# Last norm of a hybrid encoder block: the correction diagonal in one operation, gamma read from PSUM

## The chip, the cores and the metric

The kernel runs on one core of a Trainium2 chip. The time is that of the whole program on the device, in microseconds (us), as the median of three runs. Before the change the three runs took 742.75, 742.79 and 743.09 us; the median is 742.79 us.

Five engines run their own instruction streams: PE (TensorE, the matrix multiplier), DVE (VectorE), ACT (ScalarE), POOL (GpSimd) and SP (SyncE, which here only issues transfers). They wait for one another through semaphores. Matrix products land in PSUM, everything else lives in SBUF.

## The reference

One layer of a streaming encoder: two attention branches with gates, an output projection, a norm, a gated MLP with a causal convolution, and a second norm. All is float32, with 512 rows of 1024 values. What matters here is the last line:

```
def layer_norm(x, g, b):
    mu = jnp.mean(xf, axis=-1, keepdims=True)
    var = jnp.mean(jnp.square(xf - mu), axis=-1, keepdims=True)
    return ((xf - mu) * lax.rsqrt(var + LN_EPS)) * g + b
...
        x = layer_norm(DEEPNORM_ALPHA * x + h @ w_ffn_out[layer], ln2_g[layer], ln2_b[layer])
```

## The kernel before

The 512 rows are four blocks of 128 rows, x1[0] to x1[3]; a row lies on a partition, and its 1024 values are the free dimension, split in a left half (0 to 511) and a right half (512 to 1023). The FFN's second product is a scheme of seven half-size products whose partial sums are added to x1 block by block. Each product is made in float32r, as three matmuls of a high and a low part (lines 1060 to 1062). The weight of the last group is called b22_5; ACT makes its high part, whi, at L104, and DVE its low part, wlo, at L113.

Blocks 2 and 3 finish early, block 0 next, and block 1 last, with nothing left to run beside it. So block 1 has its own ending, `finish(1)`. Its left half is final at about 725 us, before its right half. At that moment DVE takes the mean of the left half alone (`near`, L1271) and computes `ahead` = (left half − near) · gamma (L1274). When the right half is there too, the true mean is known (`mv`, L1170), and the left half only needs a correction: (left − mean) · gamma = ahead + (near − mean) · gamma. PE does that sum: an identity matmul puts `ahead` in PSUM (`share_ps`, L1184), and a matmul of gamma with a diagonal matrix, whose diagonal is near − mean (`diag`, L1176), adds the correction (L1186). The two banks of `share_ps` hold quarters 0 and 1 of the row (256 values each).

The order in `finish(1)` is this. DVE makes `mv`, then `off` = −(mean − near), a 128x1 operation, then `diag` = identity · off, then `less` = (right − mean) · gamma into PSUM. POOL computes `rstd` from the variance by a power (L1172). Then come the second passes, value · rstd + beta: quarters 2, 3 and 1 on DVE (L1192, in that order), quarter 0 on ACT (`scaled`, L1188) and POOL (`r`, L1189). Each quarter goes out by its own transfer: quarters 2 and 1 from SP's queue, quarters 3 and 0 from ACT's queue (L1193, L1194). The norms of the other blocks use the same power on POOL in `norm_stats` (L835) and two passes of `scalar_tensor_tensor` on DVE with all tensors in SBUF (L839, L841).

The order of instructions on each engine is set by a scheduler that simulates the program, except where `issue_after` in the code ties one instruction behind another. Buffers rotate in pools with a fixed number of buffers: psB has four PSUM banks, psD (`bank_p`) two, psC (`bank_c`) two.

Of the kernel before, what the change touches and what calls it, by code (L numbers as in the profile page):

```python
# [11 lines left out]
F32 = mybir.dt.float32  # L12
F32R = mybir.dt.float32r
U16 = mybir.dt.uint16
AF = mybir.ActivationFunctionType
ALU = mybir.AluOpType
# [111 lines left out]
def tile_block(ctx: ExitStack, tc: tile.TileContext, xT, xN, w_qi, w_ki, w_t, w_v, w_br, w_o, w_fi, w_fo,  # L128
               bg, cw, rel, onehot, lnp, out):
    nc = tc.nc  # L130
# [4 lines left out]
    def open_pool(name, side=None, **kw):  # L135
        c = tc.tile_pool(name=name, bufs=1, side=side, **kw)
        return c, c.__enter__()

    def padded(pool, shape, dt=F32, **kw):

        n = int(np.prod(shape[1:]))
        t = pool.tile([shape[0], -(-n // 32) * 32], dt, **kw)[:, :n]
        return t if len(shape) == 2 else t.rearrange("p (a b) -> p a b", a=shape[1])
# [15 lines left out]
    def pb(name):  # L159
        return psB.tile([128, 512], F32, tag="B", name=name)  # L160
# [47 lines left out]
    for _ in range(WARM):  # L208
# [3 lines left out]
    ident = cst.tile([128, 128], F32, name="ident")  # L212
# [4 lines left out]
                            base=-383, channel_multiplier=-1)  # L217
# [604 lines left out]
    dc, dp = open_pool("dp", side="right", reuse_waits="tile")  # L822
# [6 lines left out]
    def norm_stats(r, parts):  # L829

        mv = padded(dp, [128, 2], tag="mv", bufs=2, name="mv")
        nc.vector.bn_aggr(mv, parts)
        rstd = padded(dp, [128, 1], tag="rstd", bufs=2, name="rstd")
        nc.vector.tensor_scalar(rstd, mv[:, 1:2], EPS, None, op0=ALU.add)  # L834
        nc.gpsimd.tensor_tensor(rstd, rstd, mhalf, op=ALU.pow)  # L835
        return mv, rstd

    def norm_apply(dst, r, mv, rstd, g, b, c, behind=None):
        nc.vector.scalar_tensor_tensor(dst[:, c], r[:, c], mv[:, 0:1], g[:, c], op0=ALU.subtract, op1=ALU.mult)  # L839
        with tc.issue_after(behind) if behind is not None else nullcontext():  # L840
            return nc.vector.scalar_tensor_tensor(dst[:, c], dst[:, c], rstd, b[:, c], op0=ALU.mult, op1=ALU.add).ins  # L841
# [214 lines left out]
    def product(ps, ops, part, w, c, start, stop):  # L1056

        (h, l), (wh, wl), (slot, a) = ops, w, part
        r = slice(a * 128, a * 128 + 128)
        nc.tensor.matmul(ps, h[:, slot, r], wh[:, c], start=start, stop=False)  # L1060
        nc.tensor.matmul(ps, h[:, slot, r], wl[:, c], start=False, stop=False)  # L1061
        ups["m"] = nc.tensor.matmul(ps, l[:, slot, r], wh[:, c], start=False, stop=stop).ins  # L1062
# [21 lines left out]
    def bank_c(name):  # L1084
        return psC.tile([128, 512], F32, tag="C", bufs=2, name=name)

    def bank_p(name):
        return psD.tile([128, 512], F32, tag="P", bufs=2, name=name)

    P += [bank_p(f"P{a}") for a in range(2)]  # L1090
    for f in range(2, FC):
# [12 lines left out]
        if f == 4:  # L1104
            later = [(dp.tile([128, D], F32, tag=tag, name=f"ln{row}"), row) for row, tag in ((2, "lg"), (3, "lb"))]
            g2, b2 = later[0][0], later[1][0]
# [15 lines left out]
    wc, wp = open_pool("wp", side="right", reuse_waits="tile")  # L1122
# [27 lines left out]
    left, right = slice(0, 512), slice(512, 1024)  # L1150

    def add(j, c, what, stats=None, eng=nc.vector):

        eng.tensor_add(x1[j][:, c], x1[j][:, c], what)
        if stats is not None:
            nc.vector.bn_stats(parts2[j][:, stats], x1[j][:, c])

    def finish(j, behind=None):
        r = x1[j]
        if j != 1:  # L1160
            mv, rstd = norm_stats(r, parts2[j])
            for c in (left, right):
                norm_apply(r, r, mv, rstd, g2, b2, c, behind)
                sent = (nc.scalar if j == 0 else nc.gpsimd).dma_start(out[j * 128:(j + 1) * 128, c], r[:, c])
            if j != 0:
                with tc.issue_after(sent.ins):
                    nc.gpsimd.drain()
            return
        mv = padded(dp, [128, 2], tag="mv", bufs=2, name="mv")
        nc.vector.bn_aggr(mv, parts2[j])  # L1170
        rstd = padded(dp, [128, 1], tag="rstd", bufs=2, name="rstd")
        nc.gpsimd.tensor_tensor(rstd, mv[:, 1:2], mhalf, op=ALU.pow)  # L1172
        off = padded(dp, [128, 1], name="off")
        nc.vector.tensor_scalar(off, mv[:, 0:1], near[:, 0:1], -1.0, op0=ALU.subtract, op1=ALU.mult)
        diag = wp.tile([128, 512], F32, tag="m1", bufs=2, name="diag")[:, :128]
        turned = nc.vector.tensor_scalar(diag, ident, off, None, op0=ALU.mult).ins  # L1176
        less = bank_p("less_ps")
        with tc.issue_after(turned):
            nc.vector.scalar_tensor_tensor(less, r[:, right], mv[:, 0:1], g2[:, right], op0=ALU.subtract, op1=ALU.mult)
        quarters = [slice(256 * n, 256 * n + 256) for n in range(4)]  # L1180
        shares = [bank_c(f"share_ps{n}")[:, :256] for n in range(2)]
        with tc.issue_after(behind):
            for ps, c in zip(shares, quarters):
                nc.tensor.matmul(ps, ident, ahead[:, c], start=True, stop=False)  # L1184
        for ps, c in zip(shares, quarters):
            nc.tensor.matmul(ps, diag, g2[:, c], start=False, stop=True)  # L1186
        scaled = wp.tile([128, 512], F32, tag="m1", bufs=2, name="scaled")[:, :256]
        nc.scalar.activation(scaled, shares[0], AF.Copy, scale=rstd)  # L1188
        nc.gpsimd.tensor_add(r[:, quarters[0]], scaled, b2[:, quarters[0]])  # L1189
        for n, src, eng in ((2, less[:, 0:256], nc.sync), (3, less[:, 256:512], nc.scalar), (1, shares[1], nc.sync)):  # L1190
            c = quarters[n]
            nc.vector.scalar_tensor_tensor(r[:, c], src, rstd, b2[:, c], op0=ALU.mult, op1=ALU.add)  # L1192
            eng.dma_start(out[j * 128:(j + 1) * 128, c], r[:, c])  # L1193
        nc.scalar.dma_start(out[j * 128:(j + 1) * 128, quarters[0]], r[:, quarters[0]])  # L1194
# [3 lines left out]
    def get(key):  # L1198

        w = st.get(key)  # L1200
        while st.used < len(order) and order[st.used][0] in HOLD:
            t = order[st.used][0]
            held[t] = st.get(t)
        return w
# [12 lines left out]
    m1, u2, u3 = [], [], []  # L1217
# [42 lines left out]
    for n in range(2, 6):  # L1260
        group(f"b21_{n}", A12, M2)
        if n == 3:
            for a in range(2):
                finish(2 + a, st.done["b22_0"])
# [5 lines left out]
    near = padded(dp, [128, 2], name="near")  # L1270
# [15 lines left out]
    for n in range(2):  # L1286
# [3 lines left out]
        for i in range(2 * n, 2 * n + 2):  # L1290
            c = slice(i % 2 * 512, i % 2 * 512 + 512)
            product(whole_half, rest_ops[i], (S4, 1), w, c, i == 0, i == parted - 1)
    add(1, right, whole_half)
    held["b22_5"] = get("b22_5")
    for key, w in held.items():
        group(key, S4, M3, (0,), w)
    whole = ups["m"]
    add(0, right, M3[0], 1)
    finish(0)
    for n in range(2):  # L1300
        for key, w in held.items():
            with tc.issue_after(whole):
                last_block(key, w, n)
        add(1, slice(512 + 256 * n, 768 + 256 * n), halves[n], 1 + n)
    finish(1, ups["m"])
    close(wc)
    close(fc)
# [71 lines left out]
```

## Time and profile before

| | before |
|---|---|
| median of three runs | 742.79 us |
| profiled execution | 742.96 us |
| its span, first to last instruction | 741.1 us |
| PE busy | 734.5 us, 99% |
| DVE busy | 569.7 us, 77% |
| ACT busy | 409.0 us, 55% |
| POOL busy | 153.4 us, 21% |
| granted PE clock | 1.0 |

A row of a timeline gives the start in us, the duration in us (for merged rows from the first start to the last end), the engine, the line, the operation, output<-inputs and a count. A q behind an engine's name is its sequencer, which issues transfers. A row of the groups gives busy time in us and the mean of one instruction in ns, and the idle time ahead of it.

### The profile page before, as it was taken

To read this page: it belongs to the slowest core of one execution; us is meant where nothing else is said; L and a number is where in the kernel's file an instruction comes from. 1 tells how busy PE (TensorE), PEld (TensorE's weight loads), DVE (VectorE), ACT (ScalarE), POOL (GpSimd) and SP (SyncE) were. 2 spreads that over 40 slices of the span, in tenths; PEclk is the share of its full clock that TensorE was granted. 3 is DMA by queue.
4 is the path that set the end of the run, shared out by engine and by line. 5 is a ranking of instruction groups with operands and counts; after the bars stand their busy time and mean duration, and the time that the engine had idled before them with its cause. 6 is when DMAs were issued, how large, how long until landed. Compare 5 with 4: busy or idle time off the path is not lost.

```text
span 741.1 us, 9715 instructions
## 1 busy us (share of the span) xinstructions
PE 734.5 (99%) x3445; PEld 615.1 (83%) x3445; DVE 569.7 (77%) x912; ACT 409.0 (55%) x575; POOL 153.4 (21%) x168
## 2 busy tenths in 40 slices
PE   9999999999999999999999999999999999999997
PEld 7888888888888888888889888888888888888886
DVE  5569888999679898568856876686667677668986
ACT  6466867797786688755384443443444344336430
POOL 1002224365753341000100222012101100110011
PEclk9999999999999999999999999999999999999999
DMA  8335977797566464438631554444443444447532
GB/s 281 144 127 202 204 165 173 156 211 174 126 172 164 135 142 122 124 112 263 241 64 50 174 153 150 157 160 145 149 155 115 154 146 149 137 151 279 183 136 86
DMA packets 74959, 117.29 MB, mean 158 GB/s; under 512 B 43736, under 2 KB 44248, under 8 KB 74912
## 3 DMA queue, kind: packets, MB, share of 16 engines
q1 hardware_dynamic: 67536, 94.38, 41.1%
q0 software_dynamic: 5840, 18.38, 10.3%
q10 hardware_dynamic: 1536, 3.93, 2.1%
q8 instruction: 27, 0.44, 0.2%
q14 instruction: 20, 0.16, 0.1%
HBM read 95.93 MB, written 9.98 MB: 143 GB/s over the span
## 4 chain that ended last, share of the span: by engine, by line
PE 98%; DVE 1%; DMA 0%; issue 0%; ACT 0%; POOLq 0%; POOL 0%
PE g_ps L966 16%; PE u_ps L966 16%; PE av_ps L512 3%; PE m L1062 2%; PE m L1061 2%; PE m L1060 2%; PE ga_ps L233 2%; PE ga_ps L234 2%; PE ga_ps L232 2%; PE gb_ps L234 2%; PE gb_ps L232 2%; PE gb_ps L233 2%; PE o_ps L867 2%; PE o_ps L869 2%; PE o_ps L868 2%; PE z_ps L539 1%
## 5 line engine op out<-in xcount | busy, mean ns | idle before, releaser
L104 ACT ACTIVATE whi<-raw 128x1024 fp32r<-128x1024 f32 (+1 forms) x124 | 123.5, 999 | 130.5 <-PE g_ps L966 40.0
L113 DVE TENSOR_TENSOR wlo<-raw,whi 128x1024 fp32r<-128x1024 f32 (+1 forms) x105 | 122.7, 1171 | 36.3 <-ACT whi L104 35.8
L966 PE MATMUL g_ps<-x1h,whi 128*128 128x512 f32 (+1 forms) x184 | 70.1, 381 | 0.0
L966 PE MATMUL g_ps<-x1h,wlo 128*128 128x512 f32 (+1 forms) x184 | 69.9, 380 | 0.0
L966 PE MATMUL g_ps<-x1l,whi 128*128 128x512 f32 (+1 forms) x184 | 69.9, 380 | 0.0
L966 PE MATMUL u_ps<-x1h,whi 128*128 128x512 f32 (+1 forms) x184 | 69.6, 380 | 0.0
L966 PE MATMUL u_ps<-x1h,wlo 128*128 128x512 f32 (+1 forms) x184 | 69.6, 380 | 0.0
L966 PE MATMUL u_ps<-x1l,whi 128*128 128x512 f32 (+1 forms) x184 | 68.9, 380 | 0.0
L981 DVE TENSOR_TENSOR t<-raw 128x512 f32<-128x512 f32 x11 | 7.6, 691 | 42.4 <-DMA raw<-in_w_fo_dram 42.4
L966 PEld LDWEIGHTS g_ps<-x1h,whi 128*128 128x128 f32 x184 | 34.6, 188 | 6.7 <-DVE hF L1036 0.3
L966 PEld LDWEIGHTS g_ps<-x1h,wlo 128*128 128x128 f32 x184 | 34.6, 188 | 6.6
L966 PEld LDWEIGHTS g_ps<-x1l,whi 128*128 128x128 f32 x184 | 34.6, 188 | 6.6
L966 PEld LDWEIGHTS u_ps<-x1h,wlo 128*128 128x128 f32 x184 | 34.6, 188 | 6.5
L966 PEld LDWEIGHTS u_ps<-x1h,whi 128*128 128x128 f32 x184 | 34.6, 188 | 6.5
L966 PEld LDWEIGHTS u_ps<-x1l,whi 128*128 128x128 f32 x184 | 34.3, 188 | 6.6
L567 POOL TENSOR_TENSOR bm<-win,score 128x256 f32<-128x256 f32 (+2 forms) x24 | 28.8, 1229 | 32.6 <-DMA pl<-bm 22.2
L1028 ACT ACTIVATE c<-c,cwt 128x512 f32<-128x512 f32 x22 | 15.9, 724 | 31.0 <-DVE c L1027 30.9
L1022 POOL MEMSET u<- 128x2 f32 x22 | 2.1, 98 | 139.6 <-ACT whi L104 83.0
L1036 DVE TENSOR_TENSOR hF<-g_ps,c 128x512 f32<-128x512 f32 x22 | 15.1, 686 | 16.5 <-PE g_ps L966 15.7
L835 POOL TENSOR_TENSOR rstd<-rstd,mhalf 128x1 f32<-128x1 f32 x7 | 6.8, 965 | 100.0 <-DVE rstd L834 100.0
L424 DVE MAX8 m<-score 128x8 f32<-128x256 f32 (+2 forms) x48 | 26.5, 554 | 0.9
L556 POOL TENSOR_TENSOR beta<-beta,keep 128x1280 f32<-128x1280 f32 x8 | 21.0, 2626 | 25.9 <-DVE keep L553 25.9
(598 smaller groups left out, 2089.8 us busy)
## 6 DMA issues: line engine op xcount, KB each, us to landing
raw<-in_w_fi_dram SPq DMA_DIRECT2D x44, 512.0 KB, 3.3
raw<-in_w_t_dram SPq DMA_DIRECT2D x32, 512.0 KB, 3.6
raw<-in_w_fo_dram SPq DMA_DIRECT2D x26, 512.0 KB, 4.3
wlo<-in_w_t_dram POOLq DMA_DIRECT2D x14, 512.0 KB, 6.0
raw<-in_w_br_dram SPq DMA_DIRECT2D x8, 512.0 KB, 3.8
raw<-in_w_o_dram SPq DMA_DIRECT2D x8, 512.0 KB, 3.8
raw<-in_w_v_dram SPq DMA_DIRECT2D x7, 512.0 KB, 4.4
raw_b<-in_w_fo_dram SPq DMA_DIRECT2D x6, 512.0 KB, 5.1
```

The lines of the kernel that those rows point to most:

```text
L104: self.high = nc.scalar.activation(hi[:, :w], t[:, :w], AF.Copy).ins
L113: self.done[key] = eng.tensor_sub(lo[:, :w], t[:, :w], r32(hi[:, :w])).ins
L232: nc.tensor.matmul(ps[:M], wh[:, c], xh[k], start=(k == 0), stop=False)
L233: nc.tensor.matmul(ps[:M], wh[:, c], xl[k], start=False, stop=False)
L234: ups["proj"] = nc.tensor.matmul(ps[:M], wl[:, c], xh[k], start=False, stop=(k == KC - 1)).ins
L424: nc.vector.max(m8, sc)
L512: nc.tensor.matmul(dst, vt[i][:, h].rearrange("p a d -> p (a d)"), t, start=(n == 0), stop=(n == len(seq) - 1))
L556: nc.gpsimd.tensor_mul(beta, beta, keep[:, 1:ATT + 1])
L567: nc.gpsimd.tensor_add(bm[:, OFF[j]:OFF[j] + N], win[:, 512 - N:512], score[j])
L966: nc.tensor.matmul(ps[:, c], a[:, k * 128:k * 128 + 128], b[:, k, c], start=(k == 0 and a is wh and b is x1h), stop=(n == len(terms) - 1 a ...
L1028: nc.scalar.activation(c, c, AF.Gelu_apprx_tanh, bias=cwt[:, f, 3:4])
L1036: nc.vector.tensor_mul(F[:, o:o + 2].rearrange("p a b -> p (a b)"), gps_, c)
```

## The change

`off` goes, and `diag` becomes one operation: diag = (−identity) · mean + identity · near. Its two tensors are made earlier by ACT: `minus`, the negative identity, in an SBUF buffer of the pool that `ahead` uses, and `base`, the identity times `near`, in a PSUM bank of psD. ACT also copies the right half of gamma into a PSUM bank of psB (`gamma`), and `less` reads it there in place of g2 in SBUF. `base` has the bank that `less` had, and `less` the one of the partial sum `m3_1` that was added to x1 before.

```
-        off = padded(dp, [128, 1], name="off")
-        nc.vector.tensor_scalar(off, mv[:, 0:1], near[:, 0:1], -1.0, op0=ALU.subtract, op1=ALU.mult)
         diag = wp.tile([128, 512], F32, tag="m1", bufs=2, name="diag")[:, :128]
-        turned = nc.vector.tensor_scalar(diag, ident, off, None, op0=ALU.mult).ins
+        turned = nc.vector.scalar_tensor_tensor(diag, minus, mv[:, 0:1], base, op0=ALU.mult, op1=ALU.add).ins
         less = bank_p("less_ps")
         with tc.issue_after(turned):
-            nc.vector.scalar_tensor_tensor(less, r[:, right], mv[:, 0:1], g2[:, right], op0=ALU.subtract, op1=ALU.mult)
+            nc.vector.scalar_tensor_tensor(less, r[:, right], mv[:, 0:1], gamma, op0=ALU.subtract, op1=ALU.mult)
...
     add(1, right, whole_half)
+    minus = wp.tile([128, 512], F32, tag="u2", bufs=2, name="minus")[:, :128]
+    nc.scalar.activation(minus, ident, AF.Copy, scale=-1.0)
+    base, gamma = bank_p("base_ps")[:, :128], pb("gamma_ps")
+    nc.scalar.activation(base, ident, AF.Copy, scale=near[:, 0:1])
+    nc.scalar.activation(gamma, g2[:, right], AF.Copy)
     held["b22_5"] = get("b22_5")
```

DVE's stream in `finish(1)`, before (ln_4290 is gamma, ln_4291 beta, r_3475 block 1; what a row waits for stands in brackets):

```order
L1170 BN_AGGR mv<-parts_1_6009 128x2 [waits DVE_49]
L1174 TENSOR_SCALAR off<-mv,near 128x1 [waits DVE_49]
L1176 TENSOR_SCALAR diag<-ident,off 128x128 [waits DVE_49]
L1179 SCALAR_TENSOR_TENSOR less_ps<-r_3475,mv,ln_4290 128x512
L1192 SCALAR_TENSOR_TENSOR r_3475<-less_ps,rstd,ln_4291 128x256 [waits DVE_49,Pool_49]
L1192 SCALAR_TENSOR_TENSOR r_3475<-less_ps,rstd,ln_4291 128x256
L1192 SCALAR_TENSOR_TENSOR r_3475<-share_ps_6543,rstd,ln_4291 128x256 [waits PE_49]
```

and now:

```order
L1170 BN_AGGR mv<-parts_1_6009 128x2 [waits DVE_49]
L1174 SCALAR_TENSOR_TENSOR diag<-minus,mv,base_ps 128x128 [waits DVE_49,Activation_49]
L1177 SCALAR_TENSOR_TENSOR less_ps<-r_3475,mv,gamma_ps 128x512
L1190 SCALAR_TENSOR_TENSOR r_3475<-less_ps,rstd,ln_4291 128x256 [waits DVE_49,Pool_49]
L1190 SCALAR_TENSOR_TENSOR r_3475<-less_ps,rstd,ln_4291 128x256
L1190 SCALAR_TENSOR_TENSOR r_3475<-share_ps_6547,rstd,ln_4291 128x256 [waits PE_49]
```

The row of `off` is gone, `diag` has a second semaphore to wait for, that of ACT, and the rows behind it keep their order and their waits.

ACT's stream from the high part of the weights b22_0 (`b_0h`) to the end, as a difference (whi_6392 is the high part of b22_5):

```order
 L104 ACTIVATE b_0h<-raw_b_0_6315 128x1024 [waits DMAHW6_49,DVE_49,PE_49]
+L1296 ACTIVATE gamma_ps<-ln_4290 128x512
 L104 ACTIVATE whi_6392<-raw_b_5_6350 128x512 [waits DMAHW0_49,PE_49]
+L1295 ACTIVATE base_ps<-ident,near 128x128 [waits DVE_49]
+L1293 ACTIVATE minus<-ident 128x128
 L1164 DMA out_dram<-r_3474 128x512 [waits DVE_49] x2
```

The copy of gamma has moved ahead of whi, though it stands behind `near` in the code; `base` and `minus` stand between whi and the output transfers of block 0. Of the three only `base` waits, for DVE. On PE, POOL and SP the rows and their order are as before.

## The prediction

> **What bounds the kernel now.** I read the page first, for the engine that sets the pace, then the stages of the end, then the timeline of the last eight microseconds.
>
> ```profile
> PE 734.5 (99%) x3445; PEld 615.1 (83%) x3445; DVE 569.7 (77%) x912; ACT 409.0 (55%) x575; POOL 153.4 (21%) x168
> ```
>
> PE is busy for 99% of the span, so only PE's work, or the stretch at the end where PE has none, can change the time. The change leaves PE's stream alone. The stretches (start:end, length, then busy time of PE, PEld, DVE, ACT, POOL with counts, PE clock, DMA share, GB/s) show where that end is:
>
> ```profile
> 725.00:734.00 9.00, 9.00 (x61) 8.34 (x60) 5.73 (x13) 0.00 (x0) 2.00 (x3) 1.00 0.16 60
> 734.00:738.00 4.00, 2.03 (x9) 1.12 (x7) 3.63 (x10) 0.47 (x1) 1.28 (x2) 1.00 0.36 133
> 738.00:741.00 3.00, 0.00 (x0) 0.00 (x0) 0.00 (x0) 0.00 (x0) 0.00 (x0) 0.95 0.52 172
> ```
>
> Until 734 PE has no gap; from 734 to 738 DVE is busy for 3.63 of 4.00 us and sets the pace; from 738 on only transfers and the closing run. In the middle stretch the DVE rows are:
>
> ```profile
> 734.12 0.41 DVE L1154 TENSOR_TENSOR r<-r,m 128x256 f32<-128x256 f32 x1
> 734.56 0.43 DVE L1156 BATCH_NORM_STATS2 parts<-r 128x6 f32<-128x256 f32 x1
> 735.02 0.24 DVE L1170 BATCH_NORM_AGGREGATE mv<-parts 128x2 f32<-128x18 f32 x1
> 735.30 0.21 DVE L1174 TENSOR_SCALAR off<-mv,near 128x1 f32<-128x1 f32 x1
> 735.54 0.29 DVE L1176 TENSOR_SCALAR diag<-ident,off 128x128 f32<-128x128 f32 x1
> 735.75 0.75 DVE L1179 SCALAR_TENSOR_TENSOR less_ps<-r,mv,ln 128x512 f32<-128x512 f32 x1
> 736.60 0.88 DVE L1192 SCALAR_TENSOR_TENSOR r<-less_ps,rstd,ln 128x256 f32<-128x256 f32 x2
> 737.40 0.47 DVE L1192 SCALAR_TENSOR_TENSOR r<-share_ps,rstd,ln 128x256 f32<-128x256 f32 x1
> ```
>
> and those of the other engines:
>
> ```profile
> 735.88 1.13 PE L1186 MATMUL share_ps<-ln,diag 128*128 128x256 f32 x4 [0.98 <-DVE diag L1176]
> 736.68 0.47 ACT L1188 ACTIVATE scaled<-share_ps,rstd 128x256 f32<-128x256 f32 x1 [18.57 <-PE share_ps L1186]
> 735.41 0.55 POOL L1172 TENSOR_TENSOR rstd<-mv,mhalf 128x1 f32<-128x1 f32 x1 [3.43 <-DVE mv L1170]
> 737.23 0.73 POOL L1189 TENSOR_TENSOR r<-scaled,ln 128x256 f32<-128x256 f32 x1 [1.28 <-ACT scaled L1188]
> 737.12 0.36 SPq L1193 DMA_DIRECT2D out_dram<-r  x1
> 737.90 0.34 SPq L1193 DMA_DIRECT2D out_dram<-r  x1
> 737.99 0.36 ACTq L1194 DMA_DIRECT2D out_dram<-r  x1
> ```
>
> The reader should see two branches behind `mv`. The **DVE branch** is off, diag, less, three second passes, and SP's last transfer at 737.90. The **PE branch** leaves it at diag: PE at 735.88, ACT at 736.68, POOL at 737.23, and ACT's transfer at 737.99, which is the last of the program. The DVE branch has 0.09 us of slack against it. `rstd` is there at 735.41 + 0.55 = 735.96 and isn't last for anyone: DVE's second pass begins at 736.60, 0.10 after less ended, and ACT waits for PE.
>
> **The change part by part.** *off goes.* From off's start to diag's is 735.54 − 735.30 = 0.24 us. The new diag needs `mv` as off did, so I start it at 735.30. Its other wait, ACT's `minus`, is long over (below).
>
> *diag gets dearer.* No such operation of 128x128 is in the trace; larger ones and two others of 128x128 are (group rows: busy, mean ns):
>
> ```profile
> L839 DVE SCALAR_TENSOR_TENSOR r<-r,mv,ln 128x512 f32<-128x512 f32 x12 | 8.4, 742 | 0.0
> L1192 DVE SCALAR_TENSOR_TENSOR r<-less_ps,rstd,ln 128x256 f32<-128x256 f32 x2 | 0.9, 478 | 0.1
> L584 DVE CUSTOM_DVE_ANT_0 lg<-l_ps,win 128x128 f32<-128x128 f32 x8 | 2.3, 283 | 0.0
> L594 DVE TENSOR_SCALAR lg<-lg,rs 128x128 f32<-128x128 f32 x8 | 4.9, 608 | 0.2
> ```
>
> From 512 to 256 elements the cost falls by 264 ns, so from 256 to 128 by 132: 346 ns, and L1192 reads one of its tensors from PSUM, as diag now will. The bounds are 283 ns (L584, one PSUM and one SBUF tensor of this very size) and 608 ns (L594). I take 346, from the same operation. Then diag ends at 735.30 + 0.346 = 735.65, where it ended at 735.54 + 0.286 = 735.83: **−0.18 us** (by the bounds −0.24 to +0.08). PE's first row, 0.05 behind diag, goes from 735.88 to 735.70, and with it ACT, POOL and the last transfer: 737.99 becomes 737.81.
>
> *less on DVE.* It began 0.21 after diag's start, 0.076 before diag's recorded end; the same overlap gives 735.30 + 0.346 − 0.076 = 735.57, also −0.18. It reads gamma from PSUM now. Rows with a PSUM tensor at 512, and the slowest of this operation at that size:
>
> ```profile
> L878 DVE SCALAR_TENSOR_TENSOR r<-r,o_ps 128x512 f32<-128x512 f32 x8 | 5.4, 683 | 6.8 <-PE o_ps L869 6.8
> L415 DVE SCALAR_TENSOR_TENSOR score<-relu,wi,score 128x512 f32<-128x512 f32 x7 | 6.0, 864 | 0.0
> ```
>
> L878 has no pointer scalar, which less has; so I keep less's own 754 ns, with 683 and 864 as bounds. It then ends at 736.32, the second passes start at 736.42, and SP's last transfer is at 737.72. At 864 ns it would be 737.83, 0.02 behind ACT's 737.81: the slack nearly hides it, and the sum would be −0.16. At 683 nothing more is won, since ACT's transfer is last.
>
> *rstd on POOL* starts at 735.41 as before and must now be there by 736.42 (0.18 sooner). The same power elsewhere is dearer:
>
> ```profile
> L835 POOL TENSOR_TENSOR rstd<-rstd,mhalf x7: 923/983/1008, 363.6 to 731.0; 128x1 f32<-128x1 f32 x7
> 730.81 1.40 DVE L839 SCALAR_TENSOR_TENSOR r<-r,mv,ln 128x512 f32<-128x512 f32 x2
> 731.04 0.93 POOL L835 TENSOR_TENSOR rstd<-rstd,mhalf 128x1 f32<-128x1 f32 x1 [4.35 <-DVE rstd L834]
> ```
>
> Seven times it took 0.92 to 1.01 us while DVE ran L839, whose tensors all lie in SBUF; at L1172, beside off and diag, 0.55. The first pass of L839 ends at 730.81 + 0.74 = 731.55 and the power at 731.97, 0.42 later. So the power looks held until a pass over two SBUF tensors is over. In the new order less starts 0.18 nearer to the power, which is where gamma's place counts: with a PSUM tensor less has one SBUF tensor, and so has diag. I take 0.55; even 1.01 would end at 736.42, just in time, so this term is nothing either way.
>
> The Trainium skill has a rule for this, in SBUF — State Buffer, Who interferes with whom: a DVE instruction with two SBUF inputs contends with a GpSimd instruction that reads SBUF, whichever comes first blocks the other to its end, and one with at most one SBUF input doesn't contend. The seven rows of L835 agree with it; by it the new diag and less leave the power alone, and the sum stays. But by it the power at 735.41 should also have held up the old diag, a SBUF to SBUF scaling, until 735.96; diag's row shows 0.29 us. So the rule isn't carried by every row here.
>
> *ACT's three copies.* The timeline rows around them, and last a group row for the size:
>
> ```profile
> 714.76 1.06 ACT L104 ACTIVATE b_0h<-raw_b 128x1024 fp32r<-128x1024 f32 x1 [1.66 <-DVE wlo L113]
> 717.48 0.63 ACT L104 ACTIVATE whi<-raw_b 128x512 fp32r<-128x512 f32 x1 [1.66 <-PE m L1062]
> 724.89 0.17 DVE L1271 BATCH_NORM_AGGREGATE near<-parts 128x2 f32<-128x6 f32 x1
> 728.16 0.39 PE L1060 MATMUL m<-whi,bh 128*128 128x512 f32 x1
> 733.24 1.00 ACTq L1164 DMA_DIRECT2D out_dram<-r  x2
> L587 ACT ACTIVATE lg<-lg,mn 128x128 f32<-128x128 f32 x8 | 3.1, 394 | 0.3 <-DVE mn L584 0.3
> ```
>
> gamma costs what whi of the same shape does, 0.63 us, and falls in the 1.66 us in which ACT sat idle ahead of whi: nothing. Were that cover gone, whi would come 0.63 later, and PE needs it only at 728.16. base waits for near (725.06), and takes with minus about 2 · 0.39 us (estimate from L587's row): both are done by 726.0. Behind them on ACT stand only block 0's transfers at 733.24, 7 us later, and diag needs them at 735.30. Nothing.
>
> **Sum:** −0.18 us. The profiled execution took 742.96 (span 741.1 and 1.86 around it), which becomes 742.78; that execution lies 0.17 above the median, so the median goes from 742.79 to **742.6 us**, −0.02%.
>
> **The rivals.** *A: rstd becomes late* (slower). If DVE's less holds POOL up although gamma is in PSUM, or if the power slips behind it, rstd ends 0.42 after less: 736.32 + 0.42 = 736.74. With the 0.10 gap the second passes start at 736.84, 0.24 later than before, and SP's last transfer moves from 737.90 to 738.14, 0.15 behind the old last one: 742.94. It decides once rstd comes after 736.42, and costs more than the change brings once it comes after about 736.6. For it: the seven long powers. Against it: less has one SBUF tensor, and the power starts 0.16 before it. *B: the end does not move.* The four transfers of 128 KB are what the span ends with, and DMA moves 172 GB/s in the last stretch; if their landing rather than their issue set the end, the time stays 742.8. Against it: the first of them is issued at 737.12, and from 734 to 738 the DMA share is 0.36, so nothing of an earlier stage fills the engines, and all four are issued 0.18 sooner. *C: diag is as slow as L594's row,* 608 ns: +0.08 us, 742.9, and less is late by as much. Against it: L1192 and L839 both put it near 346. *D: the edit does more than I see,* because the old diag or less paid for the power beside them: less's 754 against L839's 742 leaves 0.01 us, so 742.6 at best.
>
> **How the numbers follow.** Forecast (with D, the same time) 0.68; A 0.12; B 0.13; C 0.07. The cases lie within 742.6 to 742.94. The three runs of before spread from −0.04 to +0.30 around their median, and another set of runs need not have the same median. So the range is 742.2 (0.4 under the forecast, for bounds of −0.24 and the spread) to 743.2 (A plus the spread). A measurement of this kernel can tell about 0.2%, 1.5 us, from no change; no case comes near that in either direction, since the whole stretch behind `mv` to the last transfer is only 2.7 us long. Hence: faster by more than 0.2% 0.03, within it 0.95, slower 0.02, where what is left stands for things that the trace doesn't hold.
>
> **What would show it.** In the new profile, counted from `mv`'s start: diag 0.28 later and some 0.35 long; PE's gamma·diag matmul 0.68 later (0.86 before); the first second pass 1.40 later (1.58); ACT's last transfer 2.79 later (2.97). rstd of 0.55 us shows the power free; one near 1.0, ending 0.42 behind less, shows A, and then the idle time ahead of the second pass names POOL. A transfer issued sooner with the same end shows B. A diag above 0.53 us shows C. A gap on PE at 728.16, or whi well after 717.48, would show that ACT's copies aren't hidden, and would make the prediction wrong.

## The result, and the profile after

The changed kernel takes **750.57 us** (median of four, 750.1 to 751.21) against 742.86 for the kernel before (four runs, 742.75 to 743.09): a ratio of 1.010, with a 95% interval of 1.0088 to 1.0113. It is 7.7 us slower. The forecast was 742.6 us and no measurable change.

The profiled execution took 751.21 us, with a span of 749.4. The page's row of busy times:

```profile
PE 742.7 (99%) x3445; PEld 615.5 (82%) x3445; DVE 570.4 (76%) x911; ACT 410.6 (55%) x578; POOL 152.1 (20%) x168
```

PE runs as many instructions as before and is busy for 8.2 us longer, at the same share of 99%; in sum it waited no more, its work took longer. The stretches, cut at the first matmul of the FFN's first product (L966), at the end of its part with matmuls of 256 columns, at its last matmul, and at mv (start:end, length, then busy time of PE, PEld, DVE, ACT, POOL, PE clock, DMA share, GB/s; PEld is PE's loading of weights), before:

```profile
0.00:388.25 388.25, 386.74 (x1846) 325.03 (x1847) 310.02 (x553) 266.90 (x401) 105.57 (x95) 1.00 0.62 167
388.25:402.70 14.45, 14.45 (x111) 13.91 (x110) 7.71 (x13) 5.97 (x8) 1.01 (x3) 1.00 0.09 18
402.70:671.00 268.30, 268.30 (x1187) 222.05 (x1186) 192.54 (x255) 111.17 (x140) 40.48 (x61) 1.00 0.45 149
671.00:735.00 64.00, 63.90 (x302) 53.47 (x301) 56.73 (x84) 24.51 (x27) 5.11 (x7) 1.00 0.51 177
735.00:741.10 6.10, 1.13 (x4) 0.68 (x4) 2.67 (x7) 0.47 (x1) 1.28 (x2) 0.97 0.34 117
```

and after:

```profile
0.00:389.60 389.60, 387.98 (x1847) 325.42 (x1848) 310.49 (x553) 266.89 (x401) 104.17 (x95) 1.00 0.63 166
389.60:404.00 14.40, 14.40 (x110) 13.80 (x109) 7.71 (x13) 6.03 (x8) 1.01 (x3) 1.00 0.09 18
404.00:679.00 275.00, 275.00 (x1188) 222.25 (x1187) 192.92 (x255) 111.70 (x141) 40.51 (x61) 1.00 0.45 146
679.00:743.30 64.30, 64.15 (x302) 53.34 (x300) 56.73 (x84) 25.52 (x30) 5.11 (x7) 1.00 0.52 175
743.30:749.40 6.10, 1.13 (x4) 0.68 (x4) 2.51 (x6) 0.47 (x1) 1.27 (x2) 0.76 0.33 116
```

The last stretch, where every instruction of the change but ACT's copies lies, is 6.10 us long in both; PE's granted clock is lower in it now, but its four matmuls take 1.13 us in both. The loss sits far ahead of it: 6.7 us between about 403 and 679 us, where the same 1187 or 1188 matmuls need 275.0 us in place of 268.3, with PE busy throughout and the granted clock at 1.00; and 0.3 us in the stretch behind. The second stretch, in the main L966's matmuls of 256 columns, hasn't grown. The first stretch is 1.35 us longer in this execution; 0.8 of it is one wait of PE for a late transfer (L234 below). The other two stretches hold 7.0 of the 7.7 us between the medians; what holds the rest this one profile doesn't show. The chain of waits shows one group of 24 matmuls of 512 columns (start, length, line, count), first of before, then of after:

```profile
503.93 5.44 PE u_ps L966 x24
```

```profile
507.56 5.60 PE u_ps L966 x24
```

One of them takes 5.44 / 24 = 227 ns from start to start before, and 5.60 / 24 = 233 ns now. In the groups by line and shape, L966 has six rows of 168 with 512 columns, 1008 matmuls; one row of before and one of after, and the row of the late transfer:

```profile
L966 PE MATMUL u_ps<-x1h,whi 128*128 128x512 f32 x168 | 65.4, 389 | 0.0
```

```profile
L966 PE MATMUL u_ps<-x1h,whi 128*128 128x512 f32 x168 | 66.4, 395 | 0.0
...
L234 PE MATMUL gb_ps<-xh,wlo 128*128 128x512 f32 x64 | 24.9, 392 | 0.8 <-DMA wlo<-in_w_t_dram 0.8
```

All six rows of L966 went from 389 or 390 to 395 ns, and 1008 · 6.6 ns = 6.7 us. The same shape in the projections ahead of it (L234) is still at 392. So something about the operands of L966 has changed, and the change names none of them.

What did change is where they lie. `off` was a tile of the pool dp, one value a partition, padded to 128 bytes. With it gone, dp is 128 bytes smaller, and since the pools of the right side are stacked, dp and what is stacked against it moved up by 128 bytes. The built programs place the operands so (byte in each partition, and what is left of it on division by 256; L966 streams x1h and x1l against weights in whi and wlo):

```
            before   after    byte modulo 256, before and after
x1h         170432   170560   192   64
x1l         186816   186944   192   64
whi, wlo     29888 and on     192  192
```

So the streamed operand and the weights lay at the same place modulo 256 before, and 128 apart after. The experiments ask whether that is the cause.

### The profile page after: what moved, and what is told of

It reads as the page before. It is cut to its first block, busy times and chain, and to the rows that moved or that the text cites. A ratio compares the mean times of both kernels' runs of the same rounds, so it can differ in the third digit from the quotient of the medians.

```text
span 749.4 us, 9718 instructions
## 1 busy us (share of the span) xinstructions
PE 742.7 (99%) x3445; PEld 615.5 (82%) x3445; DVE 570.4 (76%) x911; ACT 410.6 (55%) x578; POOL 152.1 (20%) x168
## 4 chain that ended last, share of the span: by engine, by line
PE 95%; DMA 1%; issue 1%; DVE 1%; POOL 1%; ACT 1%; POOLq 0%; ACTq 0%
PE u_ps L966 16%; PE g_ps L966 16%; PE m L1060 2%; PE av_ps L512 2%; PE m L1062 2%; PE m L1061 2%; PE ga_ps L233 2%; PE ga_ps L234 2%; PE ga_ps L232 2%; PE o_ps L869 2%; PE o_ps L868 2%; PE o_ps L867 2%; PE gb_ps L234 2%; PE gb_ps L233 1%; PE gb_ps L232 1%; PE l_ps L578 1%
## 5 line engine op out<-in xcount | busy, mean ns | idle before, releaser
L966 PE MATMUL g_ps<-x1h,whi 128*128 128x512 f32 (+1 forms) x184 | 70.9, 385 | 0.0
L966 PE MATMUL g_ps<-x1h,wlo 128*128 128x512 f32 (+1 forms) x184 | 70.9, 385 | 0.0
L966 PE MATMUL g_ps<-x1l,whi 128*128 128x512 f32 (+1 forms) x184 | 70.8, 385 | 0.0
L966 PE MATMUL u_ps<-x1h,whi 128*128 128x512 f32 (+1 forms) x184 | 70.6, 385 | 0.0
L966 PE MATMUL u_ps<-x1h,wlo 128*128 128x512 f32 (+1 forms) x184 | 70.6, 385 | 0.0
L966 PE MATMUL u_ps<-x1l,whi 128*128 128x512 f32 (+1 forms) x184 | 69.9, 385 | 0.0
L966 PEld LDWEIGHTS u_ps<-x1h,whi 128*128 128x128 f32 x184 | 34.6, 188 | 7.7
L966 PEld LDWEIGHTS u_ps<-x1h,wlo 128*128 128x128 f32 x184 | 34.5, 188 | 7.6
L966 PEld LDWEIGHTS g_ps<-x1l,whi 128*128 128x128 f32 x184 | 34.5, 188 | 7.6
L966 PEld LDWEIGHTS g_ps<-x1h,wlo 128*128 128x128 f32 x184 | 34.5, 188 | 7.6
L966 PEld LDWEIGHTS g_ps<-x1h,whi 128*128 128x128 f32 x184 | 34.6, 188 | 7.5
L966 PEld LDWEIGHTS u_ps<-x1l,whi 128*128 128x128 f32 x184 | 34.3, 188 | 7.7
L567 POOL TENSOR_TENSOR bm<-win,score 128x256 f32<-128x256 f32 (+2 forms) x24 | 26.9, 1145 | 32.8 <-DMA pl<-bm 19.1
```

The source lines that it names most:

```text
L567: nc.gpsimd.tensor_add(bm[:, OFF[j]:OFF[j] + N], win[:, 512 - N:512], score[j])
L966: nc.tensor.matmul(ps[:, c], a[:, k * 128:k * 128 + 128], b[:, k, c], start=(k == 0 and a is wh and b is x1h), stop=(n == len(terms) - 1 a ...
```

## Experiments

**The bytes kept.** The changed kernel, with an unused tile of off's size in off's place:

```
+        kept = padded(dp, [128, 1], name="kept")
```

> The changed kernel, with one more tile of 128 bytes a partition in the pool dp, in the place where off lay; nothing writes or reads it. It puts x1h and x1l, the operands that stream through PE in the FFN's first product, and every other tile back on the addresses that they had before the change; the instructions are those of the changed kernel. Theory L (layout: with off's 128 bytes gone, dp and the pools under it move up by 128 bytes, and the 1008 matmuls of 512 columns that stream x1h or x1l take 233 ns from start to start in place of 227): the median goes back to the time before less what the end won, 742.7 us, and the group rows of L966 to a mean of 389 ns. Theory I (the change's own instructions, ACT's copies or gamma's PSUM bank, slow PE down): it stays near 750.5 us, L966 at 395 ns.

Measured: 743.0 us, a ratio of 1.0001 to the kernel before (0.9992 to 1.0011). All six rows of L966 are back:

```profile
L966 PE MATMUL u_ps<-x1h,whi 128*128 128x512 f32 x168 | 65.4, 389 | 0.0
```

One unused tile takes back the whole loss, with every instruction of the change still there. Theory I is out.

**The bytes taken from the kernel before.**

```
-        off = padded(dp, [128, 1], name="off")
+        off = near4[:, 2:3]
...
-    near = padded(dp, [128, 2], name="near")
+    near4 = padded(dp, [128, 4], name="near")
+    near = near4[:, 0:2]
```

> The kernel before the change, with its two operations off and diag, but off written into the unused part of near's tile, so that dp is 128 bytes smaller, as in the changed kernel. Theory L: slow without any of the change's instructions, 742.9 + 1008 x 6.4 ns = 749.4 us or somewhat more (the changed kernel lost 6.9 us from 402 us on), L966 at 395 ns. Theory I: 742.9 us, L966 at 389 ns.

Measured: 750.33 us, ratio 1.0099 (1.0084 to 1.0114), L966 as in the changed kernel:

```profile
L966 PE MATMUL u_ps<-x1h,whi 128*128 128x512 f32 x168 | 66.4, 395 | 0.0
```

The kernel before, with its own instructions in their order, is as slow as the changed one as soon as its tiles move by 128 bytes. The layout is enough to cause the loss, and by the run ahead it is needed for it.

**Which address: the streamed operand's own, or its distance from the weights?**

```
-    cst = ctx.enter_context(tc.tile_pool(name="cst", bufs=1))
+    cst = ctx.enter_context(tc.tile_pool(name="cst", bufs=1)); cst.tile([128, 32], F32, name="spare")
```

> The changed kernel, with 128 unused bytes a partition at the front of the left side's first pool, so that the weight buffers (whi, wlo) and all else on the left side move up by 128 bytes too. x1h and x1l then start 64 bytes past a multiple of 256, as in the changed kernel, and the weights do so as well, where they started 192 past one. Two forms of theory L part here. L-absolute (the streamed operand's own address decides: slow at 64 past a multiple of 256): L966 stays at 395 ns, and the FFN's second product, which streams the weights, becomes slow too, some 770 matmuls of 512 columns x 6.5 ns = 5 us: about 755.5 us. L-relative (the distance between streamed operand and weights decides: slow at 128 modulo 256): L966 goes back to 389 ns, and the early projections, whose streamed xh has not moved while their weights have, become slow, some 960 matmuls x 6.5 ns = 6.2 us: about 749 us.

Measured: 748.05 us, ratio 1.0068 (1.0053 to 1.0083). The rows of L966 and of a projection (L232, xh streamed against whi), of before and of this run:

```profile
L966 PE MATMUL g_ps<-x1l,whi 128*128 128x512 f32 x168 | 65.4, 389 | 0.0
L232 PE MATMUL ga_ps<-xh,whi 128*128 128x512 f32 x64 | 25.0, 391 | 0.0
```

```profile
L966 PE MATMUL g_ps<-x1l,whi 128*128 128x512 f32 x168 | 65.4, 389 | 0.0
L232 PE MATMUL ga_ps<-xh,whi 128*128 128x512 f32 x64 | 25.3, 395 | 0.0
```

L966 is fast again although x1h and x1l lie where they lie in the changed kernel; what has moved is the left side, the weights with it. And the projections, whose streamed xh hasn't moved while their weights have, became slow. That is L-relative; L-absolute asked for the opposite at both places. The time came out 1 us under the 749 expected: the projections pay 4 to 5 ns each, not 6.5.

**A period of 256 bytes?** x1h and x1l moved by 256 bytes in place of 128 (near put in the unused part of a statistics tile of dp, which takes 128 more bytes out of the pool):

```
+    parts3 = dp.tile([128, 32], F32, name="parts2_3")
...
-    near = padded(dp, [128, 2], name="near")
+    near = parts3[:, 16:18]
```

> The changed kernel, with near in the unused part of another small tile of dp, so that x1h and x1l lie 256 bytes above their old addresses in place of 128. Theory L with a period of 256 bytes: fast again, 742.7 us, L966 at 389 ns. Theory L with any move being bad, or a period of 512 bytes or more: 750 us, L966 at 395 ns. Theory I: 750.5 us.

Measured: 742.94 us, ratio 0.9996 (0.9987 to 1.0006), L966 at 389 ns again. A move as such isn't harmful; one by 256 bytes changes nothing.

**Between 0 and 256.** The changed kernel with 64 or 96 unused bytes in dp, and with 64 unused bytes and near moved as above: distances of 64, 32 and 192 bytes.

```
-        nc.gpsimd.tensor_tensor(rstd, mv[:, 1:2], mhalf, op=ALU.pow)
+        nc.gpsimd.tensor_tensor(rstd, mv[:, 1:2], mhalf, op=ALU.pow); dp.tile([128, 16], F32, name="kept")
```

That is the edit for 64 bytes; for 96 the tile is `[128, 24]`.

> The changed kernel with 64 unused bytes a partition in dp in place of off's 128: x1h and x1l lie 64 bytes above their old place, so streamed operand and weights are 64 apart, modulo 256. What the distance costs is open; three shapes. Proportional to the distance from 0 modulo 256: half of what 128 cost, 742.9 + 3.5 = 746.4 us, L966 at 392 ns. Any distance but 0 costs the whole: 749.9 us, 395 ns. Only 128 costs: 742.9 us, 389 ns.

> The same with 96 unused bytes in dp: a distance of 32 bytes. Proportional: a quarter, 744.6 us, L966 at 390.5 ns. Any distance: 749.9 us, 395 ns. Only 128: 742.9 us, 389 ns.

> near in the unused part of another tile of dp and 64 unused bytes kept: x1h and x1l lie 192 bytes above their old place. Proportional and symmetric about 128: as at 64, 746.4 us. Growing with the distance up to 256: 742.9 + 10 = 753 us. Any distance: 749.9 us. Only 128: 742.9 us.

Measured: 746.26 us at 64 (ratio 1.0037, 1.0027 to 1.0047), 750.66 at 32 (1.0092, 1.0074 to 1.011), 749.72 at 192 (1.0081, 1.0063 to 1.0099). One row of L966 at 32, one at 192, and three at 64:

```profile
L966 PE MATMUL u_ps<-x1h,whi 128*128 128x512 f32 x168 | 66.4, 395 | 0.0
```

```profile
L966 PE MATMUL u_ps<-x1h,whi 128*128 128x512 f32 x168 | 66.2, 394 | 0.0
```

```profile
L966 PE MATMUL g_ps<-x1h,whi 128*128 128x512 f32 x168 | 66.2, 394 | 0.0
...
L966 PE MATMUL g_ps<-x1h,wlo 128*128 128x512 f32 x168 | 65.8, 392 | 0.0
L966 PE MATMUL g_ps<-x1l,whi 128*128 128x512 f32 x168 | 65.3, 389 | 0.0
```

None of the three shapes holds: the proportional one fits the 746.4 us that it gave for 64 bytes, and misses at 32 and 192. 32, 128 and 192 cost about the whole, 64 well under half; and at 64 the matmuls don't pay alike: those that stream x1l pay nothing, and of those with x1h the ones ahead of them pay most. Averaged over L966's matmuls of 512 columns, from start to start, these take 226.8, 233.4, 229.1, 233.3, 233.3 and 226.7 ns at 0, 32, 64, 128, 192 and 256 bytes. What within PE or SBUF makes it isn't shown by any of these runs, and stays open.

**Only x1h and x1l put back.** 128 unused bytes at the end of their own pool; dp and wp stay 128 bytes higher:

```
-    x1l = qp.tile([128, KC, S], F32R, name="x1l")
+    x1l = qp.tile([128, KC, S], F32R, name="x1l"); qp.tile([128, 32], F32, name="spare")
```

> The changed kernel with 128 unused bytes at the end of the pool that holds x1h and x1l alone: these two are back on their old addresses, while dp (the norm's tiles, x1, gamma, beta) and later wp (weights of the last groups, diag, ahead, minus) stay 128 bytes higher. If the 1008 matmuls of L966 carry the whole loss, 742.7 to 743.0 us with L966 at 389 ns; the matmuls of the last groups that stream weights held in wp may still cost some 6 ns each, 100 to 200 of them, 0.6 to 1.2 us, and would bring it to 743.5 to 744 us. If x1's or the norm's place mattered: near 750 us.

Measured: 743.78 us, against 743.27 for the kernel before beside it, ratio 1.0006 (0.9996 to 1.0016): no difference that can be told. L966 is at 389 ns. The few matmuls of the last groups that stream weights held in wp are still slow; one of their rows (t3_1, low part), of before and of this run, and in this run the row of t3_2, whose weights lie in a pool that hasn't moved:

```profile
L1061 PE MATMUL m<-t_1l,bh 128*128 128x512 f32 x4 | 1.6, 389 | 0.0
```

```profile
L1061 PE MATMUL m<-t_1l,bh 128*128 128x512 f32 x4 | 1.6, 396 | 0.0
...
L1061 PE MATMUL m<-t_2l,bh 128*128 128x512 f32 x4 | 1.6, 390 | 0.0
```

So within one run, on one line and for one shape, the rows whose operands lie 128 bytes apart are the slow ones. The built program has 54 of these matmuls in place of the 100 to 200 that were expected, so 54 · 6 ns = 0.3 us: the 0.3 us that the changed kernel also lost behind L966. L966 carries the rest.

**The change's two parts apart.** With the addresses of before: the changed kernel with gamma left in SBUF and no copy of it, then the kernel before with gamma in PSUM, off and diag as they were.

```
-    base, gamma = bank_p("base_ps")[:, :128], pb("gamma_ps")
+    base, gamma = bank_p("base_ps")[:, :128], g2[:, right]
...
-    nc.scalar.activation(gamma, g2[:, right], AF.Copy)
```

```
-            nc.vector.scalar_tensor_tensor(less, r[:, right], mv[:, 0:1], g2[:, right], op0=ALU.subtract, op1=ALU.mult)
+            nc.vector.scalar_tensor_tensor(less, r[:, right], mv[:, 0:1], gamma, op0=ALU.subtract, op1=ALU.mult)
...
+    gamma = pb("gamma_ps")
+    nc.scalar.activation(gamma, g2[:, right], AF.Copy)
```

> The changed kernel with off's 128 bytes kept, and less reading gamma from SBUF as before; diag in one operation. From the start of mv (L1170) to the start of ACT's last output transfer it took 2.97 us before the change and 2.84 in the changed kernel's profile. Theory H (the power on POOL is held up while DVE runs an operation over two SBUF tensors, and less now starts nearer to it): rstd takes up to 1.0 us and ends 0.42 us after less, the first second pass starts 0.1 us later still, and the stretch is 3.1 us. Theory N (gamma's place doesn't matter, since the power has read its operands by then): rstd 0.55 us, the stretch 2.84 us. The total is within 0.5 us of 742.9 either way.

> The kernel before the change, with gamma's right half copied to PSUM by ACT and read there by less; off and diag as before, all addresses in SBUF as before. Both theories: rstd 0.55 us, less 0.75 us, the stretch from mv to ACT's last output transfer 2.97 us as before: nothing won without the shorter diag. The total is within 0.5 us of 742.9.

Measured: 743.06 us for both, each in one execution. The timeline of the first (diag alone), from mv (brackets: how long the engine was idle, and what ended that):

```profile
735.21 0.24 DVE L1170 BATCH_NORM_AGGREGATE mv<-parts 128x2 f32<-128x18 f32 x1
735.55 0.35 DVE L1174 SCALAR_TENSOR_TENSOR diag<-minus,mv,base_ps 128x128 f32<-128x128 f32 x1
735.81 0.75 DVE L1177 SCALAR_TENSOR_TENSOR less_ps<-r,mv,ln 128x512 f32<-128x512 f32 x1
735.59 0.55 POOL L1172 TENSOR_TENSOR rstd<-mv,mhalf 128x1 f32<-128x1 f32 x1 [3.44 <-DVE mv L1170]
738.05 0.36 ACTq L1192 DMA_DIRECT2D out_dram<-r  x1
```

The stretch from mv to ACT's last transfer is 2.84 us and rstd takes 0.55, with gamma in SBUF: theory N. In the second run (gamma alone) the stretch is 737.96 − 734.99 = 2.97 us, as before. So the one-operation diag brings all of the gain at the end, and gamma's place brings nothing.

**Where the gain at the end went.** The last output transfer is issued 0.12 us sooner after mv (2.97 and 2.84 are rounded), and yet the last stretch is 6.10 us long before and after. With diag alone it is 741.2 − 735.2 = 6.00. Two runs, again with the addresses of before: ACT's copy of gamma is made, and less doesn't read it; and the copy is made by DVE.

```
-            nc.vector.scalar_tensor_tensor(less, r[:, right], mv[:, 0:1], gamma, op0=ALU.subtract, op1=ALU.mult)
+            nc.vector.scalar_tensor_tensor(less, r[:, right], mv[:, 0:1], g2[:, right], op0=ALU.subtract, op1=ALU.mult)
```

```
-    nc.scalar.activation(gamma, g2[:, right], AF.Copy)
+    nc.vector.tensor_copy(gamma, g2[:, right])
```

> As the run with diag in one operation alone (off's 128 bytes kept, less reading gamma from SBUF), but ACT still makes the copy of gamma in PSUM, which nothing reads. In every profile with all three of ACT's new copies the last output lands 0.12 us sooner after mv's start than before the change (5.01 for 5.14 us), and the program still ends 6.10 us after it, because ACT's drain in the closing run comes late; with two of the copies (diag alone) or one (gamma alone) it doesn't. Theory R (the count of ACT's instructions decides, three more are too many): the end is at 6.10 us, ACT's closing drain late. Theory G (reading gamma from PSUM decides): the end is at 6.00 us, as with diag alone. The total is within 0.5 us of 742.9 either way.

> The changed kernel with off's 128 bytes kept, and the copy of gamma to PSUM made by DVE in place of ACT, so that ACT has two instructions more than before and less still reads gamma from PSUM. Theory R: the program ends 6.00 us after mv's start. Theory G: 6.10 us. The last output transfer is issued 2.85 us after mv's start by both. The total is within 0.5 us of 742.9.

Measured, each in one execution: 744.34 us for the first, 1.4 above what was expected of its total (the kernel before took 743.74 beside it; 1.25 us of the excess had built up ahead of L966, which began at 389.50 us in place of 388.25), and 743.09 for the second. From mv to the end of the span it is 6.11 us with three copies on ACT, and 5.99 with gamma copied by DVE: theory R. ACT's two DRAIN instructions in the closing run, behind the kernel's own work (count: ns least/median/most, first and last start in us), of the kernel before, of the changed kernel, of the run with three copies and less reading SBUF, and of the run with DVE's copy:

```profile
L1375 ACTq DRAIN  x2: 8/79/150, 738.4 to 740.6; - x2
```

```profile
L1378 ACTq DRAIN  x2: 135/143/151, 746.5 to 749.0; - x2
```

```profile
L1378 ACTq DRAIN  x2: 137/144/150, 739.6 to 742.1; - x2
```

```profile
L1378 ACTq DRAIN  x2: 8/79/150, 738.5 to 740.7; - x2
```

With three instructions more on ACT its last drain takes 135 or 137 ns and comes late; with two more, or none, it takes 8. The other profiles agree: in all nine with the three copies the shorter of the two drains is 122 to 137 ns long and the span ends 6.09 to 6.11 us after mv; in the two with the new diag and two copies it is 8 ns and 5.99 or 6.00 us. That gives back the 0.1 us which the shorter diag had won. Why the third instruction does it, the runs don't show.

## Why the prediction was wrong

The step that failed is the first, "The change leaves PE's stream alone", and what was concluded from it, that only the end can change the time. The rows of PE's stream are the same, one by one, but how long a row takes changed: 1008 matmuls went from 227 to 233 ns from start to start. The step "off goes" counted off's instruction and its 0.24 us, and not its 128 bytes, which hold x1h and x1l where they are. No rival had it, and so the chance of 0.02 for a loss above 0.2%, and the top of the range at 743.2 us, were wrong. None of the rows that I had read said that these matmuls could be slower; that the two kernels place their tiles differently could have been read from the two programs.

The other steps, in their places:

- *Off and diag.* These rows of the changed kernel answer to those of before:

```profile
743.30 0.24 DVE L1170 BATCH_NORM_AGGREGATE mv<-parts 128x2 f32<-128x18 f32 x1
743.64 0.35 DVE L1174 SCALAR_TENSOR_TENSOR diag<-minus,mv,base_ps 128x128 f32<-128x128 f32 x1
743.91 0.75 DVE L1177 SCALAR_TENSOR_TENSOR less_ps<-r,mv,gamma_ps 128x512 f32<-128x512 f32 x1
744.76 0.88 DVE L1190 SCALAR_TENSOR_TENSOR r<-less_ps,rstd,ln 128x256 f32<-128x256 f32 x2
743.68 0.55 POOL L1172 TENSOR_TENSOR rstd<-mv,mhalf 128x1 f32<-128x1 f32 x1 [3.43 <-DVE mv L1170]
746.14 0.36 ACTq L1192 DMA_DIRECT2D out_dram<-r  x1
```

  diag takes 0.35 us, as the line through 512 and 256 elements gave; rival C is out. But it starts 0.34 us after mv's start, not 0.28, in every profile that has it. It has a second semaphore to wait for, ACT's, which off hadn't, and the built program has a waiting instruction of its own ahead of diag for that; that this is the reason wasn't tried apart from the operation itself. It took 0.06 of the 0.18: second passes at 1.46 after mv (1.40 forecast, 1.58 before), ACT's last transfer at 2.84 (2.79 forecast, 2.97 before). The gain at the last transfer was 0.12 us.
- *less* kept its 0.75 us with gamma in PSUM, as taken.
- *rstd* took 0.55 us; rival A did not come. The reason given for gamma's place, that less over two SBUF tensors would hold the power up, fell too: in the run with diag alone less reads gamma from SBUF, and rstd takes 0.55 us all the same. There the power had begun 0.22 us ahead of less; in the seven long ones the DVE pass began first. Nor did the power, having begun first, hold less up, whose 0.75 us began 0.32 us before the power's end. The rows of before had shown as much: less, with two tensors in SBUF, began at 735.75 and took 0.75 us, and the power ran from 735.41 to 735.96. The prediction looked for this at the old diag instead. That has only one tensor in SBUF, and so isn't a case of two engines in each other's way as the prediction describes it.
- *ACT's three copies* ran where forecast, hidden from PE and DVE, but not free: as three instructions more they cost the closing run 0.1 us. So the end did not move, which is rival B's outcome by another mechanism than B's; the landing of the transfers was not its cause.
- *Sum:* with the bytes kept, the change is worth 743.0 against 742.96 us, 1.0001 (0.9992 to 1.0011). Apart from the layout, the forecast of no measurable change held; that says little for its 0.18 us, which these medians can't resolve and of which the end of the span kept next to nothing (6.10 us from mv, before and after).

The Trainium skill, in SBUF — State Buffer, Who interferes with whom, gives PE two independent read ports, one for the streamed operand and one for the weights, and says that PE and ACT never wait on anyone. By that the distance between the two couldn't matter; the runs differ, at 227 ns for a distance of 0 or 256 bytes and 233 for 128.

Left open: what the distance does within the chip, and why 64 bytes cost about a third of what 32 do; whether other types pay as well. Of the shapes, 256 columns paid nothing: the stretch that is in the main L966's matmuls of them took 14.45 us before and 14.40 after, though their operands moved apart too. The last groups' and the projections' matmuls of 512 columns paid at 128 bytes, 4 to 7 ns each.

## What to carry to other kernels

A change that adds or removes a tile, however small, moves every tile stacked behind it; compare the addresses of the two programs as well as their instructions, and look at the mean of PE's groups first when a loss shows in a stretch that wasn't edited. Here a kernel whose PE is never idle gains or loses 1% by 128 bytes: when a tile goes, keep its bytes, or move by 256 (both measured at no change). A comparison of two edits is fair only with the same layout.

## What the runs showed of the hardware that was not expected

- A float32r matmul of 512 columns on 128 by 128 weights goes from 227 to 233 ns from start to start when its streamed operand and its weights lie 128 bytes apart modulo 256; at a distance of 0 or 256 it doesn't (1008 matmuls, 389 and 395 ns in their rows, granted clock 1.00 in both). At 32, 64 and 192 bytes it costs 6.6, 2.3 and 6.5 ns in the mean, and matmuls of 256 columns paid nothing at 128.
- diag in one operation, which waits for a second semaphore, of an engine that was long done, started 0.34 us after mv's start (eleven profiles), where off, with one semaphore, started after 0.27 to 0.28 (three). The two operations differ as well, so the wait isn't shown to be the cause.
- Three more instructions on ACT, hidden beside other work, made its last drain 122 to 137 ns long in place of 8 (nine profiles), and the closing run 0.1 us longer; two more did not (two profiles).
- A power on POOL that had begun 0.22 us earlier did not hold up a DVE pass over two SBUF tensors: 0.55 and 0.75 us in the run with diag alone, where the seven powers that began behind such a pass took 0.92 to 1.01.
